# Weight block sums by adding transfers, four plain pairs first, and token operands in portions

## Chip, cores and metric

One core of a Trainium2 chip runs the whole program. The metric is the device time in microseconds (us), as the median of several executions. TensorE (PE in the profile) multiplies matrices, VectorE (DVE) and ScalarE (ACT) work element by element, GpSimd (POOL) too, and SyncE (SP) issues transfers between DRAM and the on-chip memory.

## What is computed

A two-layer bidirectional encoder trunk on 512 + 256 tokens with a model width of 1024. Each layer has a mixer (layer 0: HGRN2 and dilated window attention; layer 1: gated linear attention), then a gated convolutional feed-forward network (FFN), then a per-layer embedding added through a sigmoid gate. The change lies in the FFN alone, which runs once per layer:

```python
def _conv_ffn(x, w_up, conv_w, conv_b, w_down):   # x: RMS-normed, 1024 wide; w_up: 1024 x 5632
    u = x @ w_up
    up = jnp.pad(u, ((0, 0), (1, 1), (0, 0)))
    u = up[:, :-2] * conv_w[0] + up[:, 1:-1] * conv_w[1] + up[:, 2:] * conv_w[2] + conv_b
    a, gate = jnp.split(u, 2, axis=-1)
    return (a * jax.nn.gelu(gate, approximate=False)) @ w_down
```

## The kernel before

Activations lie transposed: 128 features on the partitions, the 768 tokens along a row. Every fp32 matrix product is made of three products of rounded parts: a value v is split into hi = round(v), made by ACT, and lo = v - hi, made by DVE, and TensorE adds w_hi x_hi, w_hi x_lo and w_lo x_hi.

Weights come in slabs of 128 x 1024 floats (512 KB) in a fixed list (`slabs`, built by `tail` at L1119 for the FFN). `prep` (L55) loads the next slab with SP (L72), makes hi on ACT (L73) and lo on DVE (L74). `slab` (L163) hands out a prepared slab and prepares one ahead. The tiles `raw`, `whi` and `wlo` have two buffers each, so hi and lo of a slab can be written when the products of the slab before the last are done. `proj` (L179) multiplies one slab with all tokens: 8 blocks x 3 parts x (512 + 256 columns), 48 matmuls in `gemm` (L177).

The up projection of the FFN needs 22 pairs of feature tiles, a linear one and a gate. The first NSTD = 2 pairs are plain: two slabs each, by `proj`, with evacuation into u on DVE (L965), times the norm factor R, which arrives late, after the first slab. The other 20 pairs use a Strassen-Winograd form of the 2 x 2 block product (two feature tiles, two halves of the 1024 inputs, two halves of the tokens) with seven products in place of eight: `seven` (L111), 7 x 12 = 84 matmuls of 386 columns each (L119), into three PSUM banks x, y, z. It needs

- sums of weight blocks: `prep_pair` (L78) loads two slabs (L81, L83), makes S1 and S3 on POOL (L97, L98), S2 and S4 on DVE (L99, L100), then splits the seven blocks in four operations on ACT and four on DVE (L90, L91);
- sums of token blocks: `operands(p)` (L933) scales two tiles of h by gain and R on DVE (L938) and calls `seven_operands` (L146): differences t1, t2 on DVE (L150, L152), t3, t4 on POOL (L151, L153), then four splits on ACT and DVE (L156, L157). It is called whole after each of the four plain projections, and a product of `seven` needs all four sets.

In `seven`, ACT copies the first and third product out (p1 L127, p5 L133), POOL adds them (L134), DVE makes u2 (L130), and four additions write u (L975, L978), after which POOL clears the gap columns between the two token groups (L977). `activate` (L953) follows whole: per half one ACT operation and two DVE taps (L947 to L950), Gelu on ACT, a product on DVE (L959). The down projection comes next: it splits each of the 22 results (`split`, L226, L227) and multiplies them in two passes of 11 slabs.

A scheduler makes each engine's instruction order at compile time, mainly by the order in the program among what it holds to be ready; an engine then runs its list strictly in that order. `bg` holds background generators; `tick`, called after each block or product, runs them on.

Of the kernel before, what the change touches and what calls it, by code (L numbers as in the profile page):

```python
# [13 lines left out]
ALU = mybir.AluOpType  # L14
# [21 lines left out]
HC = AC // 2  # L36
NSTD = 2
# [8 lines left out]
class Net:  # L46
# [8 lines left out]
    def prep(self, cut=1024, ahead=None):  # L55
        if self.sp >= len(self.slabs):
            return
        src = self.slabs[self.sp]
        self.sp += 1
        n = src.shape[-1]  # L60
        nc = self.nc
        if n == 2048:
            self.ready.append(self.prep_pair(src))
            return
# [12 lines left out]

    def prep_pair(self, src):  # L78
        nc = self.nc
        ra = self.wp.tile([128, 1024], F32, tag="raw", name="ra")  # L80
        nc.sync.dma_start(out=ra, in_=src[:, 0:1024])  # L81
        rb = self.wp.tile([128, 1024], F32, tag="raw", name="rb")
        nc.sync.dma_start(out=rb, in_=src[:, 1024:2048])  # L83
        a11, a12, a22, a21 = ra[:, 0:512], ra[:, 512:1024], rb[:, 0:512], rb[:, 512:1024]

        def parts(hpool, htag, lpool, ltag, r):
            n = r.shape[-1]
            hi = hpool.tile([128, 1024], F32R, tag=htag, bufs=2, name=htag)[:, :n]
            lo = lpool.tile([128, 1024], F32R, tag=ltag, bufs=2, name=ltag)[:, :n]
            nc.scalar.activation(hi, r, AF.Copy)  # L90
            nc.vector.tensor_tensor(out=lo, in0=r, in1=hi.bitcast(F32), op=ALU.subtract)  # L91
            return [[(hi[:, c:c + 128], lo[:, c:c + 128]) for c in range(c0, c0 + 512, 128)]
                    for c0 in range(0, n, 512)]
        sa = self.fp.tile([128, 1024], F32, tag="S", bufs=2, name="sa")
        sb = self.fp.tile([128, 1024], F32, tag="S", bufs=2, name="sb")
        s2, s1, s3, s4 = sa[:, 0:512], sa[:, 512:1024], sb[:, 0:512], sb[:, 512:1024]
# [4 lines left out]
        w = {}  # L101
        w["A11"], w["A12"] = parts(self.wp, "whi", self.wp, "wlo", ra)
        w["S2"], w["S1"] = parts(self.fp, "hs", self.fp, "ls", sa)
        w["S3"], w["S4"] = parts(self.fp, "hs", self.fp, "ls", sb)
        w["A22"], = parts(self.wp, "whi", self.wp, "wlo", rb[:, 0:512])
        return w
# [4 lines left out]
    def seven(self, X, c11, add):  # L111
        nc = self.nc
        W = self.slab()
        x, y, z = None, None, None
# [7 lines left out]
        pt = self.rp.tile([128, AC], F32, tag="Rt", name="p15")  # L122
        ug = self.rp.tile([128, AC], F32, tag="sq", name="ug")
        p1, p5, u2, g = pt[:, 0:HC], pt[:, HC:AC], ug[:, 0:HC], ug[:, HC:AC]
        x = self.mm()[:, 0:HC]
        prod(x, "A11", "B11", True)
        nc.scalar.copy(p1, x)  # L127
        y = self.mm()[:, 0:HC]
        prod(y, "S2", "T2", True)
        nc.vector.tensor_tensor(out=u2, in0=y, in1=p1, op=ALU.add)  # L130
        z = self.mm()[:, 0:HC]
        prod(z, "S1", "T1", True)
        nc.scalar.copy(p5, z)  # L133
        nc.gpsimd.tensor_tensor(out=g, in0=p1, in1=p5, op=ALU.add)  # L134
        prod(x, "A12", "B21", False)
        c11(x)
        prod(y, "S3", "T3", False)
        add(1, 1, y, g)
        prod(z, "S4", "B22", False)
        add(0, 1, z, u2)  # L140
        prod(y, "A22", "T4", False)
        add(1, 0, y, p1)
# [3 lines left out]
    def seven_operands(self, x1, x2, ta, tb, slots):  # L146
        nc = self.nc
        b11, b12, b21, b22 = x1[:, 0:HC], x1[:, HC:AC], x2[:, 0:HC], x2[:, HC:AC]
        t1, t2, t3, t4 = ta[:, 0:HC], ta[:, HC:AC], tb[:, 0:HC], tb[:, HC:AC]
        nc.vector.tensor_tensor(out=t1, in0=b12, in1=b11, op=ALU.subtract)  # L150
        nc.gpsimd.tensor_tensor(out=t3, in0=b22, in1=b12, op=ALU.subtract)  # L151
        nc.vector.tensor_tensor(out=t2, in0=b22, in1=t1, op=ALU.subtract)  # L152
        nc.gpsimd.tensor_tensor(out=t4, in0=b21, in1=t2, op=ALU.subtract)  # L153
        s11, h2, l2, ha, la, hb, lb = slots
        for hi, lo, v in ((s11[:, 0:HC], s11[:, HC:AC], b11), (ha, la, ta), (h2, l2, x2), (hb, lb, tb)):
            nc.scalar.activation(hi, v, AF.Copy)  # L156
            nc.vector.tensor_tensor(out=lo, in0=v, in1=hi.bitcast(F32), op=ALU.subtract)  # L157
        self.X["B11"].append((s11[:, 0:HC], s11[:, HC:AC]))
        for names, h, lo in ((("B21", "B22"), h2, l2), (("T1", "T2"), ha, la), (("T3", "T4"), hb, lb)):
            self.X[names[0]].append((h[:, 0:HC], lo[:, 0:HC]))  # L160
            self.X[names[1]].append((h[:, HC:AC], lo[:, HC:AC]))
# [748 lines left out]
    def ffn(self, l):  # L910
        nc, tc, a = self.nc, self.tc, self.a
        with tc.tile_pool(name=f"f{l}", bufs=1) as fp, \
# [10 lines left out]
            for k in range(KT):  # L923
                nc.sync.dma_start(out=hd[k], in_=self.h[k])
            for u in us:
# [4 lines left out]
            self.X = {n: [] for n in ("B11", "B21", "B22", "T1", "T2", "T3", "T4")}  # L930


            def operands(p):  # L933
                x1, x2 = aslot(2, f"xn{2 * p}", F32), aslot(3, f"xn{2 * p + 1}", F32)
                for k, x in ((2 * p, x1), (2 * p + 1, x2)):
                    nc.gpsimd.memset(x[:, TP:TP + GAP], 0.0)
                    for (c0, w), (uc, _) in zip(CH, ACOL):
                        nc.vector.scalar_tensor_tensor(out=x[:, uc:uc + w], in0=self.h[k][:, c0:c0 + w],  # L938
                                                       scalar=self.cols[:, C_FFN + 8 * l + k:C_FFN + 8 * l + k + 1],
                                                       in1=self.R[:, c0:c0 + w], op0=ALU.mult, op1=ALU.mult)  # L940
                tags = [(self.xp, f"x{p}"), (fp, f"xb{p}")] + [(self.xp, f"x{4 + 3 * p + i}") for i in range(3)] \
                    + [(self.hp, f"h{2 * p + i}") for i in range(2)]
                self.seven_operands(x1, x2, aslot(4, "ta", F32), aslot(5, "tb", F32),
                                    [pool.tile([128, AC], F32R, tag=t, name=t) for pool, t in tags])

            def conv_taps(c, u, f):
                nc.scalar.activation(c, u[:, 1:1 + AC], AF.Identity, scale=conv[:, f, 1:2], bias=conv[:, f, 3:4])  # L947
                nc.vector.scalar_tensor_tensor(out=c, in0=u[:, 0:AC], scalar=conv[:, f, 0:1], in1=c, op0=ALU.mult,
                                               op1=ALU.add)
                nc.vector.scalar_tensor_tensor(out=c, in0=u[:, 2:2 + AC], scalar=conv[:, f, 2:3], in1=c,  # L950
                                               op0=ALU.mult, op1=ALU.add)

            def activate(j, u):  # L953
                act[j] = aslot(j, f"act{j}", F32)
                c = fp.tile([128, AC], F32, tag="c", name="cg")
                conv_taps(act[j], u[0], j)
                conv_taps(c, u[1], NF + j)
                self.other(c, c, AF.Gelu)
                nc.vector.tensor_tensor(out=act[j], in0=act[j], in1=c, op=ALU.mult)  # L959
            for j in range(NSTD):  # L960
                for part in range(2):
                    n = 2 * j + part
                    pj = self.proj0(split=True) if n == 0 else self.proj()
# [3 lines left out]
                    if part == 1:  # L967
                        activate(j, us)
                    operands(n)
            for j in range(NSTD, NF):  # L970
                u = us

                def add(m, half, bank, other):
                    o = u[m][:, 1 + half * HC:1 + (half + 1) * HC]
                    nc.vector.tensor_tensor(out=o, in0=bank, in1=other, op=ALU.add)  # L975
                    if half:
# [286 lines left out]
```

## Time and profile before

| | us |
|---|---|
| median of 3 runs | 2387.71 |
| lowest and highest | 2387.23, 2389.49 |
| the profiled execution | 2386.55 |
| its span (first to last instruction) | 2384.8 |
| TensorE busy in it | 2291.9 |
| mean granted TensorE clock in it | 0.985 of full |

In the rows, an engine's busy time is the time in which it runs anything; "idle before" is the wait just ahead of an instruction, with the instruction that ended it. A name such as L99 is a line of the kernel. A granted clock of 1.00 is 2.4 GHz and of 0.50 is 1.2 GHz.

### The profile page before, as it was taken

Reading aid. Unit: us, or ns where it says so; the run is one execution under the profiler, and the core shown is the slowest. Engines: PE = TensorE matmul, PEld = TensorE weight load, DVE = VectorE, ACT = ScalarE, POOL = GpSimd, SP = SyncE. Lnnn points to the kernel's source line nnn. Section 1 sums busy time; section 2 is a strip of 40 time slices with the busy share of each in tenths; the row PEclk is TensorE's granted clock in tenths of the full one; section 3 lists DMA queues with packets and bytes.
Section 4 is the critical chain, followed back from the end, with each engine's and each line's share of the span. In section 5 each row is a group of like instructions: output and inputs, shape, how many; then the busy total and the mean of one; then the engine's idle time right before and its main releaser. Section 6 shows DMA issues by size and latency. Waiting matters only on the chain. (4 is left out here: it accounts for less than half of the span.)

```text
span 2384.8 us, 32943 instructions
## 1 busy us (share of the span) xinstructions
PE 2291.9 (96%) x13524; PEld 2083.2 (87%) x13524; DVE 1571.4 (66%) x2054; ACT 1052.1 (44%) x1422; POOL 247.6 (10%) x308
## 2 busy tenths in 40 slices
PE   8999999999995999999999999999968999999997
PEld 6989889898884999998888899998858999988887
DVE  7546355364548888895445687876478898864366
ACT  5333243332434454454334565655344555543353
POOL 1010010100103222220000000000032222200000
PEclk9999999999998999999999999999989999999999
DMA  4111111112230121223122311113311221231221
GB/s 160 54 54 36 54 45 45 54 45 73 93 107 31 63 69 64 71 71 115 62 76 76 106 54 36 36 36 113 111 44 54 71 71 64 70 115 65 75 87 53
DMA packets 50231, 165.70 MB, mean 69 GB/s; under 512 B 5696, under 2 KB 7744, under 8 KB 50080
## 3 DMA queue, kind: packets, MB, share of 16 engines
q1 hardware_dynamic: 48928, 162.02, 20.3%
q8 instruction: 106, 1.74, 0.3%
q10 hardware_dynamic: 1152, 1.57, 0.2%
q14 instruction: 45, 0.37, 0.1%
HBM read 150.99 MB, written 12.58 MB: 69 GB/s over the span
## 5 line engine op out<-in xcount | busy, mean ns | idle before, releaser
L177 PE MATMUL pj<-xh,whi 128*128 128x512 f32 (+1 forms) x2160 | 576.8, 348 | 9.2 <-ACT whi L73 6.1
L177 PE MATMUL pj<-xh,wlo 128*128 128x512 f32 (+1 forms) x2160 | 555.8, 339 | 22.0 <-DVE wlo L74 22.0
L177 PE MATMUL pj<-xl,whi 128*128 128x512 f32 (+1 forms) x2160 | 556.1, 338 | 2.7 <-DVE xl L233 2.7
L177 PEld LDWEIGHTS pj<-xh,wlo 128*128 128x128 f32 (+1 forms) x2160 | 331.6, 189 | 70.7 <-DVE wlo L74 22.7
L177 PEld LDWEIGHTS pj<-xl,whi 128*128 128x128 f32 (+1 forms) x2160 | 333.3, 189 | 52.6 <-DVE xl L233 4.5
L177 PEld LDWEIGHTS pj<-xh,whi 128*128 128x128 f32 (+1 forms) x2160 | 333.5, 190 | 50.7 <-ACT whi L73 6.1
L73 ACT ACTIVATE whi<-raw 128x1024 fp32r<-128x1024 f32 (+1 forms) x164 | 170.7, 1041 | 405.5 <-PE pj L177 387.6
L74 DVE TENSOR_TENSOR wlo<-raw,whi 128x1024 fp32r<-128x1024 f32 (+1 forms) x164 | 199.7, 1218 | 148.4 <-ACT whi L73 148.3
L119 PE MATMUL mm<-x,hs 128*128 128x386 f32 x800 | 221.7, 342 | 4.5 <-ACT hs L90 3.7
L119 PE MATMUL mm<-x,whi 128*128 128x386 f32 x480 | 139.8, 345 | 20.2 <-DVE x L157 15.8
L119 PEld LDWEIGHTS mm<-x,hs 128*128 128x128 f32 x800 | 147.9, 190 | 6.1 <-ACT hs L90 4.4
L227 DVE TENSOR_TENSOR xl<-act,xh 128x772 fp32r<-128x772 f32 x88 | 84.6, 968 | 69.3 <-ACT xh L226 69.3
L226 ACT ACTIVATE xh<-act 128x772 fp32r<-128x772 f32 x88 | 73.8, 843 | 95.4 <-PE pj L177 90.9
L119 PE MATMUL mm<-x,ls 128*128 128x386 f32 x320 | 109.5, 342 | 0.0
L119 PEld LDWEIGHTS mm<-x,whi 128*128 128x128 f32 x480 | 89.9, 191 | 21.9 <-DVE x L157 16.3
L357 ACT COPY kc<-X 128x768 f32<-128x768 f32 x56 | 50.5, 901 | 124.6 <-PE mm L344 68.2
L119 PE MATMUL mm<-h,whi 128*128 128x386 f32 x320 | 86.4, 351 | 17.4 <-DVE u L975 17.3
L99 DVE TENSOR_TENSOR sa<-sa,ra 128x512 f32<-128x512 f32 x40 | 69.7, 1743 | 44.2 <-POOL sa L97 44.2
L177 PE MATMUL mm<-xl,whi 128*128 128x512 f32 x352 | 90.6, 337 | 0.0
L177 PE MATMUL mm<-xh,whi 128*128 128x512 f32 x352 | 90.6, 337 | 0.0
L177 PE MATMUL mm<-xh,wlo 128*128 128x512 f32 x352 | 90.4, 338 | 0.0
L372 DVE COPY_PREDICATED A<-masks,mm 128x512 f32<-128x512 uint8 x112 | 60.8, 591 | 37.0 <-PE mm L344 36.9
(279 smaller groups left out, 4185.5 us busy)
## 6 DMA issues: line engine op xcount, KB each, us to landing
raw<-w_ev SPq DMA_DIRECT2D x55, 512.0 KB, 3.5
raw<-w_dn SPq DMA_DIRECT2D x44, 512.0 KB, 3.5
ra<-w_up SPq DMA_DIRECT2D x40, 512.0 KB, 3.7
rb<-w_up SPq DMA_DIRECT2D x40, 512.0 KB, 3.7
raw<-w_od SPq DMA_DIRECT2D x24, 512.0 KB, 3.4
hd<-h SPq DMA_DIRECT2D x24, 384.0 KB, 2.3
h<-hd SPq DMA_DIRECT2D x24, 384.0 KB, 5.3
raw<-w_pg SPq DMA_DIRECT2D x16, 512.0 KB, 3.5
```

The source lines that it names most:

```text
L73: nc.scalar.activation(hi[:, s], raw[:, s], AF.Copy)
L74: nc.vector.tensor_tensor(out=lo[:, s], in0=raw[:, s], in1=hi[:, s].bitcast(F32), op=ALU.subtract)
L99: nc.vector.tensor_tensor(out=s2, in0=s1, in1=a11, op=ALU.subtract)
L119: nc.tensor.matmul(bank, w, v, start=start and n == 0 and i == 0, stop=n == 3 and i == 2, skip_group_check=True)
L177: nc.tensor.matmul(o, w, x[:, c0:c0 + n], start=first and si == 0, stop=last and si == 2)
L226: nc.scalar.activation(xh[:, :n], src, AF.Copy)
L227: nc.vector.tensor_tensor(out=xl[:, :n], in0=src, in1=xh[:, :n].bitcast(F32), op=ALU.subtract)
L357: nc.scalar.copy(dst.rearrange("p (n c j) -> p n c j", c=2, j=h), src)
L372: nc.vector.copy_predicated(A[:, tl[0]:tl[0] + n, :], self.masks[:, li, :].unsqueeze(1).to_broadcast([128, n, 128]), p.rearrange("p (i t) ...
```

## The change

NSTD becomes 4 and HC, the half of the tokens, 384 instead of 386: the halves are now taken without the gap, and the second half is written into u in two pieces (128 and 256 columns).

Plain slabs of the up projection (tuples in the list): ACT makes hi and also -hi into lo, and a GpSimd transfer adds the slab from DRAM to lo.

Pairs: the weights are stored as four blocks of 128 x 512 (256 KB). `load_pair` loads two of them, and GpSimd transfers with `accum_op=ALU.add` form S1, S2, S3 and S4 in place, one after another in the same two buffers, each after the split of what lay there. The signs change so that sums suffice (N1, N2, N4 for T1, T2, T4); the gate half then comes out negated, which `nconv`, a negated copy of its taps, undoes. `split_pair` is a generator that splits one block per step; `split_step` takes a step after each product, so that blocks of the next pair are made during the products of this one. The order of products is now A11, S1, S2, A12, S3, S4, A22, and g is made on DVE straight from PSUM.

Token operands: `operands` scales h in place, in whole rows, makes all four differences on DVE, and yields between portions; `chain` runs it in the background, one portion for every two ticks from the second plain projection on. `activate` is a generator too, which runs during the next pair's products. The GpSimd descriptor memory goes from 1024 to 4096 bytes.

```diff
@@ prep
+        added = type(src) is tuple
...
             nc.sync.dma_start(out=raw[:, s], in_=src[:, s])
             nc.scalar.activation(hi[:, s], raw[:, s], AF.Copy)
-            nc.vector.tensor_tensor(out=lo[:, s], in0=raw[:, s], in1=hi[:, s].bitcast(F32), op=ALU.subtract)
+            if added:
+                nc.scalar.activation(lo[:, s], raw[:, s], AF.Copy, scale=-1.0)
+                nc.gpsimd.dma_start(out=lo[:, s], in_=src[:, s], accum_op=ALU.add)
+            else:
+                nc.vector.tensor_tensor(out=lo[:, s], in0=raw[:, s], in1=hi[:, s].bitcast(F32), op=ALU.subtract)
...
-        nc.gpsimd.tensor_tensor(out=s1, in0=a21, in1=a22, op=ALU.add)
-        nc.gpsimd.tensor_tensor(out=s3, in0=a11, in1=a21, op=ALU.subtract)
-        nc.vector.tensor_tensor(out=s2, in0=s1, in1=a11, op=ALU.subtract)
-        nc.vector.tensor_tensor(out=s4, in0=a12, in1=s2, op=ALU.subtract)
...
+    def load_pair(self, src):
+        r = self.wp.tile([128, 1024], F32, tag="raw", name="ra")
+        a, s = r[:, 0:512], r[:, 512:1024]
+        nc.sync.dma_start(out=s, in_=src[2])
+        nc.sync.dma_start(out=a, in_=src[0])
+        nc.gpsimd.dma_start(out=s, in_=src[3], accum_op=ALU.add)
+        return src, a, s
...
+    def split_pair(self, load, w):
+        src, a, s = load
+        a12 = self.load_block(src[1])
...
+            nc.scalar.activation(hi, r, AF.Copy)
             nc.vector.tensor_tensor(out=lo, in0=r, in1=hi.bitcast(F32), op=ALU.subtract)
...
+        parts("S1", s, 0, 0)
+        nc.gpsimd.dma_start(out=s, in_=src[0], accum_op=ALU.add)
+        yield
+        parts("A11", a, 0, 1)
+        nc.gpsimd.dma_start(out=a, in_=src[2], accum_op=ALU.add)
+        yield
+        parts("A12", a12, None, 0)
+        a22 = self.load_block(src[3])
+        yield
+        parts("S2", s, None, 0)
+        nc.gpsimd.dma_start(out=s, in_=src[1], accum_op=ALU.add)
+        yield
+        parts("S3", a, 1, 0)
+        yield
+        parts("S4", s, 1, 1)
+        yield
+        parts("A22", a22, None, 0)
+        yield
...
+    def next_pair(self):
+        self.psplit = None
+        if self.ploads:
+            w = {}
+            self.pw.append(w)
+            self.psplit = self.split_pair(self.ploads.pop(0), w)
+            if self.psrc:
+                self.ploads.append(self.load_pair(self.psrc.pop(0)))
...
+    def seven(self, c11, add):
+        def after():
             self.tick()
+            self.split_step()
...
             for j in range(NSTD):
                 for part in range(2):
                     n = 2 * j + part
+                    if n == 1:
+                        self.spawn(chain())
+                    if n == 2 * NSTD - 1:
+                        self.pairs([a["w_up2"][l, i] for i in range(NSTD, NF)])
                     pj = self.proj0(split=True) if n == 0 else self.proj()
...
                     if part == 1:
-                        activate(j, us)
-                    operands(n)
+                        run(activate(j, us, False))
+            self.drain()
+            for _ in range(5):
+                self.split_step()
             for j in range(NSTD, NF):
...
+                self.seven(lambda bank: nc.scalar.copy(us[0][:, 1:1 + HC], bank), add)
+                self.spawn(activate(j, us, True))
+            self.drain()
```

## Rows read from the trace of the kernel before

**Rows 1.** The page: busy time (share) by engine, TensorE's busy tenths in 40 slices.

```profile
PE 2291.9 (96%) x13524; PEld 2083.2 (87%) x13524; DVE 1571.4 (66%) x2054; ACT 1052.1 (44%) x1422; POOL 247.6 (10%) x308
...
PE   8999999999995999999999999999968999999997
```

**Rows 2.** Windows of both up projections: length, busy us (instructions) by engine, clock, DMA.

```profile
core 0: us, PE busy (x) PEld busy (x) DVE busy (x) ACT busy (x) POOL busy (x), PEclk, DMA share, GB/s
702.60:784.00 81.40, 55.56 (x276) 48.01 (x276) 63.79 (x82) 34.92 (x43) 25.18 (x21) 0.83 0.13 43
784.00:1081.40 297.40, 287.67 (x1604) 281.92 (x1603) 266.05 (x289) 152.83 (x198) 73.89 (x94) 1.00 0.21 68
1725.20:1800.00 74.80, 49.72 (x244) 42.37 (x243) 60.77 (x79) 32.65 (x40) 23.66 (x19) 0.82 0.12 41
1800.00:2101.20 301.20, 293.56 (x1637) 287.80 (x1636) 269.41 (x293) 155.47 (x200) 75.38 (x96) 1.00 0.21 69
```

**Rows 3.** Windows without a TensorE wait: one in the pairs, one in plain slabs.

```profile
1835.80:1850.40 14.60, 14.60 (x83) 14.60 (x84) 12.56 (x14) 7.31 (x10) 3.92 (x4) 1.00 0.23 72
1100.00:1260.00 160.00, 160.00 (x917) 139.73 (x916) 65.89 (x70) 54.04 (x62) 0.00 (x0) 1.00 0.20 68
```

**Rows 4.** TensorE's waits from 640 to 1300 us: us in total, times, longest.

```profile
PE pj L177 <- DVE wlo L74: 11.0, 1, 11.0
PE mm L119 <- DVE u L975: 9.7, 18, 1.7
PE mm L119 <- DVE x L157: 7.9, 1, 7.9
```

**Rows 5.** DVE's timeline at layer 0's head: start, us, operation [idle before <- releaser].

```profile
702.96 0.95 DVE L476 TENSOR_TENSOR h<-h,pj 128x768 f32<-128x768 f32 x1 [4.47 <-PE pj L177]
...
717.60 1.02 DVE L965 TENSOR_TENSOR u<-pj,R 128x512 f32<-128x512 f32 x2
...
740.30 0.96 DVE L157 TENSOR_TENSOR h<-tb,h 128x772 fp32r<-128x772 f32 x1 [2.75 <-ACT h L156]
741.18 1.22 DVE L74 TENSOR_TENSOR wlo<-raw,whi 128x1024 fp32r<-128x1024 f32 x1
```

**Rows 6.** POOL's timeline there: the subtraction ahead of that wait.

```profile
733.69 4.72 POOL L151 TENSOR_TENSOR tb<-xn,xn 128x386 f32<-128x386 f32 x1 [8.07 <-DVE xn L938]
```

**Rows 7.** DVE's groups from 800 to 1060 us: busy us, mean ns | idle before.

```profile
L99 DVE TENSOR_TENSOR sa<-sa,ra 128x512 f32<-128x512 f32 x17 | 29.9, 1762 | 19.8 <-POOL sa L97 19.8
L959 DVE TENSOR_TENSOR act<-act,cg 128x772 f32<-128x772 f32 x17 | 27.6, 1626 | 0.0
...
L948 DVE SCALAR_TENSOR_TENSOR act<-u,conv,act 128x772 f32<-128x772 f32 x17 | 17.3, 1020 | 0.8 <-ACT act L947 0.6
...
L975 DVE TENSOR_TENSOR u<-mm,ug 128x386 f32<-128x386 f32 x32 | 16.3, 548 | 0.0
L91 DVE TENSOR_TENSOR wlo<-rb,whi 128x512 fp32r<-128x512 f32 x17 | 11.8, 692 | 2.0 <-ACT whi L90 1.1
```

**Rows 8.** DVE's groups from 717 to 769 us, the head of layer 0.

```profile
L157 DVE TENSOR_TENSOR x<-xn,xb 128x772 fp32r<-128x772 f32 x3 | 2.9, 956 | 0.0
L965 DVE TENSOR_TENSOR u<-pj,R 128x512 f32<-128x512 f32 x4 | 2.7, 687 | 0.0
...
L959 DVE TENSOR_TENSOR act<-act,cg 128x772 f32<-128x772 f32 x2 | 1.9, 954 | 0.0
...
L965 DVE TENSOR_TENSOR u<-pj,R 128x256 f32<-128x256 f32 x4 | 1.7, 417 | 0.0
```

**Rows 9.** ACT's groups of splits over the span, by shape.

```profile
L73 ACT ACTIVATE whi<-raw 128x1024 fp32r<-128x1024 f32 x159 | 168.2, 1058 | 402.4 <-PE pj L177 384.4 <-issue 16.7 <-PE mm L177 1.0
...
L90 ACT ACTIVATE whi<-rb 128x512 fp32r<-128x512 f32 x40 | 25.3, 633 | 19.8 <-PE mm L119 19.6
```

**Rows 10.** DMA issues: count, KB each, median us from issue to landing.

```profile
ra<-w_up SPq DMA_DIRECT2D x40, 512.0 KB, 3.7
...
h<-hd SPq DMA_DIRECT2D x24, 384.0 KB, 5.3
...
yT<-y SPq DMA_DIRECT2D x4, 256.0 KB, 2.2
```

More of the change, by code (lines that the diff above doesn't have):

```diff
@@ L105, in prep_pair @@
-        w["A22"], = parts(self.wp, "whi", self.wp, "wlo", rb[:, 0:512])
-        return w
-    def seven(self, X, c11, add):
+            w[name] = [(hi[:, c:c + 128], lo[:, c:c + 128]) for c in range(0, 512, 128)]
+        parts("S1", s, 0, 0)
[6 more added lines that the diff above has]
+        a22 = self.load_block(src[3])
@@ L112, in seven, with split_step @@
+    def split_step(self):
+        if self.psplit is not None and next(self.psplit, 0) == 0:
+            self.next_pair()
+            if self.psplit is not None:
+                next(self.psplit)
+            elif self.slabs[self.sp] is None:
+                self.sp += 1
+                self.prep()
+    def seven(self, c11, add):
         nc = self.nc
-        W = self.slab()
-        x, y, z = None, None, None
+        X, W = self.X, self.pw.pop(0)
         def prod(bank, a, b, start):
@@ L125, in seven @@
         x = self.mm()[:, 0:HC]
         prod(x, "A11", "B11", True)
-        nc.scalar.copy(p1, x)
-        y = self.mm()[:, 0:HC]
[L129 to L134, printed above, removed]
+        nc.scalar.copy(q1, x)
+        after()
+        z = self.mm()[:, 0:HC]
+        prod(z, "S1", "N1", True)
@@ L135, in seven @@
+        nc.vector.tensor_tensor(out=g, in0=z, in1=q1, op=ALU.add)
+        after()
+        y = self.mm()[:, 0:HC]
+        prod(y, "S2", "N2", True)
+        nc.vector.tensor_tensor(out=u2, in0=y, in1=q1, op=ALU.add)
+        after()
         prod(x, "A12", "B21", False)
         c11(x)
+        after()
         prod(y, "S3", "T3", False)
         add(1, 1, y, g)
+        after()
         prod(z, "S4", "B22", False)
         add(0, 1, z, u2)
-        prod(y, "A22", "T4", False)
-        add(1, 0, y, p1)
+        after()
@@ L146, in seven_operands @@
+        prod(y, "A22", "N4", False)
+        add(1, 0, y, q1)
+        after()
     def seven_operands(self, x1, x2, ta, tb, slots):
         nc = self.nc
[L148 to L152, printed above, removed]
@@ new lines, in seven_operands @@
+        yield
+        nc.vector.tensor_tensor(out=t3, in0=b22, in1=b12, op=ALU.subtract)
+        nc.vector.scalar_tensor_tensor(out=n4, in0=n2, scalar=-1.0, in1=b21, op0=ALU.mult, op1=ALU.subtract)
+        high(hb, tb)
+        yield
+        low(s11[:, 0:HC], s11[:, HC:T], b11)
+        low(h2, l2, x2)
+        yield
+        low(ha, la, ta)
+        low(hb, lb, tb)
+        yield
+        self.X["B11"].append((s11[:, 0:HC], s11[:, HC:T]))
+        for names, h, lo in ((("B21", "B22"), h2, l2), (("N1", "N2"), ha, la), (("T3", "N4"), hb, lb)):
@@ new lines, in operands, with conv_taps @@
+                tags = [(self.xp, f"x{4 * p + i}") for i in range(4)]
+                tags += [(self.hp, f"h{2 * p - 2 + i}") if p else (fp, f"xb{4 + i}") for i in range(2)]
+                tags.append((fp, f"xb{p}"))
+                yield from self.seven_operands(
+                    hs[0], hs[1], aslot(4, "ta", F32)[:, :T], aslot(5, "tb", F32)[:, :T],
+                    [lambda pool=pool, t=t: pool.tile([128, T], F32R, tag=t, name=t) for pool, t in tags])
+            def conv_taps(c, u, w, f, bias):
+                nc.scalar.activation(c, u[:, 1:1 + AC], AF.Identity, scale=w[:, f, 1:2], bias=bias)
+                yield
+                for o, i in ((0, 0), (2, 2)):
+                    nc.vector.scalar_tensor_tensor(out=c, in0=u[:, o:o + AC], scalar=w[:, f, i:i + 1], in1=c,
+                                                   op0=ALU.mult, op1=ALU.add)
+                    yield
@@ new lines, in activate @@
+            def activate(j, u, negated):
+                act[j] = aslot(j, f"act{j}", F32)
+                if negated:
+                    c = self.hp.tile([128, AC], F32, tag="h6", name="cg")
+                else:
+                    c = self.rp.tile([128, AC], F32, tag="sq", name="cg")
+                gbias = conv[:, NF + j, 3:4]
+                gate = conv_taps(c, u[1], *((nconv, j, gbias) if negated else (conv, NF + j, gbias)))
+                lin = conv_taps(act[j], u[0], conv, j, conv[:, j, 3:4])
+                next(gate), next(lin)
+                for g in (lin, gate):
+                    for _ in g:
+                        yield 1
@@ L958, in activate, with run, chain @@
                 self.other(c, c, AF.Gelu)
+                yield 1
                 nc.vector.tensor_tensor(out=act[j], in0=act[j], in1=c, op=ALU.mult)
+            def run(gen):
+                for _ in gen:
+                    pass
+            def chain():
+                for p in range(KT // 2):
+                    for _ in operands(p):
+                        yield 2
             for j in range(NSTD):
```

123 lines of the change are left out of this document (54 added, 69 removed).

## Prediction

> **What bounds the kernel now.** Read the page's shares first: TensorE is busy nearly all the time and the other engines are not, so a saving elsewhere counts only where TensorE waits or runs at half clock. The slices show two such places besides the ends: the 13th slice, and the 30th and 31st [rows 1]. Then windows over each layer's up projection, cut from where the last output projection leaves TensorE to the first down matmul: the hole is at the head, with a granted clock of 0.83 and 0.82, and behind it comes a long stretch at full clock in which DVE is busy 266 of 297 us and ACT only 153 [rows 2].
>
> TensorE's price of work comes from stretches without a hole: 160 us hold 917 matmuls of alternately 512 and 256 columns, so 0.1745 us each and 48 x 0.1745 = 8.37 us per plain slab; 14.6 us hold 83 of 386 columns, so 0.176 us each and 84 x 0.176 = 14.8 us per pair of slabs in the seven-product form [rows 3]. The losses of the four windows of rows 2 follow. Layer 0's head has 276 matmuls, 192 of the four plain slabs and 84 of pairs: 33.5 + 14.8 = 48.3 us of work in 81.4 us, lost 33.1. Layer 1's head: 244, so 33.5 + 52 x 0.176 = 42.7 in 74.8, lost 32.1. The rest: 1604 x 0.176 = 282.3 in 297.4, lost 15.1; 1637 x 0.176 = 288.1 in 301.2, lost 13.1. In all 93.4 us: 65.2 in the heads (waiting, and running slowly after waiting), 28.2 in the steady stretches.
>
> Who causes them? In layer 0 TensorE waits 11.0 us for one weight remainder (wlo, L74), 7.9 us for the last token operand (L157), and 18 times about half a microsecond for an addition into u (L975) [rows 4]; layer 1 has the same three. The late wlo had its input long before, but stands on DVE behind a whole call of operands(), which waits for ACT, which waits for a POOL subtraction of 4.72 us [rows 5, 6]. In the steady stretch DVE is held by the same engine: L99 takes 1.76 us where a 512-column operation of its kind takes 0.69, L959 1.63 where it takes 0.95 without POOL beside it [rows 7, 8].
>
> **The change, part by part.** Arithmetic on TensorE: four plain slabs more and two pairs fewer per layer, and 384 columns for 386 (between the two prices of rows 3, whose pair of 512 and 256 averages 384 too: 0.1752). Needed before 4 x 8.37 + 20 x 14.78 = 329.2; after 8 x 8.37 + 18 x 84 x 0.1752 = 67.0 + 264.9 = 331.9. This costs 2.7 us per layer, 5.4 in all, and is on the path. With every wait gone the gain is 93.4 - 5.4 = 88.0 us, and the time 2387.7 - 88.0 = 2299.7. (Profiled execution: 2386.55, of which 2384.8 is span; 1.2 below the median of three, so differences are simply taken from the median.)
>
> Plain slabs. The DVE subtraction (1.22 us, rows 5) goes; ACT makes a negated copy (1.06 us, rows 9), and a GpSimd transfer of 512 KB adds the weights to it. For slab n+1 this starts when slab n starts, since the two hi and lo buffers come free then: two ACT operations 2.1 us, then the transfer, and 8.37 us until TensorE wants it. So it is hidden up to X of about 6.0 us from issue to landing. No accumulating transfer and none issued by GpSimd is in the trace. Bounds: 3.7 us, a plain load of that size, and twice that, 7.4, since its target is read as well; I take 5.3, the row of a slow load in company [rows 10]. One ACT operation ahead in the queue (about 1 us) then makes it 0.3 late, 2 us per layer for seven slabs; at 7.4 it is 2.4 late, 17 us per layer. What the removal costs if this cover fails is just that. Behind a waiting GpSimd queue stand only later accumulations, as its subtractions and memsets are gone.
>
> Heads. DVE's work there, by row durations [rows 7, 8, 5]: eight evacuations of 0.69 + 0.42, 8.8 us; four activations of 4 x 1.02 + 0.95, 20.1; four operand sets, each two scalings, four 384-column differences at 0.55 and remainders of 0.55 + 3 x 0.96 (about 7.6), 30.6. Sum 59.5, startable at 717.6, when R is there [rows 5]; without the last activation and evacuation, 53.4, so done by about 771.0. The eight plain slabs last until 702.6 + 67.0 = 769.6. The operands are cut into portions in the order of the projections, so an evacuation stands behind at most four portions, and no POOL result is waited for any more. So the 11.0 and 7.9 us go, and with them the low clock. What is late next: the first pair's blocks, behind DVE's last work of the stage: 0 to 6 us, I take 3.
>
> Steady stretch. DVE per pair: before 1.76 + 0.69 + three remainders of 1.22 and one of 0.69 + four additions of 0.55 + taps 4.08 + 1.63 = 14.7 of a 15.6 us period (14.8 of work and 15.1 lost over 19 pairs). After: seven remainders of 0.69, four PSUM additions of which two are cut into 128 and 256 columns (together 2 x 0.55 + 0.55 + 2 x 0.70), taps 4.08, product 0.95: 12.9 of 14.7 us. ACT gets shorter, more operations, at 0.63 [rows 9], and is half idle. The new thing is a chain through one buffer: load S1's block, add, split S1, add, split S2, add, split S4. The step of S2 comes three products (6.3 us) after that of S1, S4's two products (4.2 us) after S2's. A split takes 0.63 + 0.69 = 1.3 us; let a 256 KB accumulation take L from readiness to landing, with GpSimd's issue in it. Bounds: 2.2, a one-way transfer of that size, and 7.4 [rows 10] (GpSimd's price for issuing is not shown, which is why the upper end stays). I take twice 2.2, 4.4. Then S4's split waits 1.3 + 4.4 - 4.2 = 1.5 us at the head of ACT's queue, DVE's remainder behind it, and then q1, u2 and the additions that free PSUM. TensorE wants S4 only at product six, 10 us later, and an addition has one product, 2.1 us, of slack; DVE has 14.7 - 12.9 = 1.8 us to catch up. So it is covered, barely: 0 to the present 0.7 us per pair, I take 0.15, 2.7 us per layer.
>
> The rule of the Trainium skill for this price (DMA: Bandwidth & Descriptors, Anatomy of one DMA) is a fixed 2.0 us plus bytes over 436 GB/s for a GpSimd-issued transfer, that is 2.6 us for 256 KB and 3.2 for 512 KB as estimates by that page. By it neither chain waits, the residue falls to the first-pair delay and the tail, and the sum would be 2308; no run so far shows such a transfer.
>
> Small edits: the gap memsets leave POOL, which nobody misses. Scaling h in place waits for its store to DRAM, issued with the last output projection, 14 us ahead of R [rows 5]. The activations spread over the next pair's products give u back after four of seven ticks; u is written again from product four on. The down projection's first operand slots now come free at the last pair's product six instead of one: one product hides about 2 us of ACT and DVE, I take 1 us per layer (0 to 3).
>
> Sum per layer: 2 + 3 + 2.7 + 1 = 8.7, for two 17.4. **Forecast 2299.7 + 17.4 = 2317 us.** With all upper ends, 2 x (17 + 6 + 13 + 3) = 78 us: 2378.
>
> **The rivals.** (1) Nothing waits: 2296 to 2305. For it: every step has slack on paper, and 2.2 is a shown time. Against: four places with under 2 us to spare. (2) The accumulations land late but not very (X and L near 7): 7.4 costs 34 us in the plain slabs and perhaps 20 in pairs: 2335 to 2383. For it: GpSimd needs 4.72 us for one 386-column subtraction in rows 6, and its queue issues all of these in order. (3) Slower: the chain becomes the period. There are two raw buffers, so one load (3.7), three splits (3.9) and three accumulations must fit in two pairs: 7.6 + 3L = 2P. It bounds TensorE from L = 7.3 us on; the gain is used up where 67 + 6 + 18P equals the present 377 (mean of 378.8 and 376.0), P = 16.9, so from L = 8.7 us. At 10 us P is 18.8 and the time 2388 + 36 x 1.9 = 2456. Against it: 8.7 is more than twice the time of a 512 KB load. The same page's rule to move 1 MiB or more per DMA (Rules for kernel authors) also speaks against cutting two 512 KB loads into eight transfers: its fixed 2.0 us eight times is 16 us per pair if none overlaps, an estimate near this rival; the DMA share of 0.21 in rows 2 says that the engines themselves have room. (4) It doesn't do what it says: the order on DVE and ACT still puts a block behind long waits, so a head keeps half its loss. That is again 2335 to 2365 and is counted in (2).
>
> **How the numbers follow.** Forecast case, 2305 to 2335: 0.56. Rival 1: 0.12. Rivals 2 and 4: 0.15. Within 0.2% of 2387.7 (plus or minus 4.8 us, about what can be told from no change): 0.03. Rival 3: 0.14. Faster is 0.56 + 0.12 + 0.15 = 0.83. The range 2296 to 2365 holds the first two and two thirds of the third, 0.78.
>
> **What would show it.** Right: heads without a TensorE wait over 3 us, granted clock 1.0 in them, no DVE row of 1.7 us, a period per pair near 14.9 us, and up projections near 341 us (before 378.8 and 376.0). Wrong: TensorE waiting for a transfer into wlo in each plain slab (X); ACT waiting for a transfer at S4 or S2 for more than 4 us and a period above 15.6 (L); or the first pair waiting over 6 us for DVE (order).

## The result, and the profile after

The changed kernel takes 2418.03 us, the median of four runs (2413.81 to 2424.18), beside 2387.52 of the kernel before on the same chip: a ratio of 1.0128, with a 95% interval of 1.0105 to 1.0151. It is slower, by 1.3%. The profiled run, the longest of the four, took 2424.18 us, of which 2422.4 are span.

The page of the kernel after, as in [rows 1] (busy time, share and instructions by engine; TensorE's busy tenths in 40 slices), with the GpSimd queue's packets, MB and share of the 16 DMA engines, and two groups of DMA issues with the median us from issue to landing:

```profile
PE 2309.7 (95%) x13572; PEld 2083.5 (86%) x13572; DVE 1455.3 (60%) x2166; ACT 1042.1 (43%) x1492; POOL 188.9 (8%) x236
...
PE   8999999999999888889999999999998888899997
...
q0 software_dynamic: 23040, 46.15, 12.1%
...
ra<-w_up POOLq DMA_DIRECT2D x144, 256.0 KB, 4.3
...
wlo<-w_up POOLq DMA_DIRECT2D x16, 512.0 KB, 7.6
```

The 5 and the 6 of [rows 1] are gone. In their place TensorE runs at 8 tenths all through the pairs. The work that was to be taken off DVE is off it (1455.3 us of busy time for 1571.4 before), and the kernel is longer all the same.

Windows over layer 0's up projection, with the columns of [rows 2]: the eight plain slabs, the 18 pairs, and a stretch inside the pairs.

```profile
703.30:777.70 74.40, 70.83 (x390) 60.61 (x389) 57.49 (x81) 41.95 (x51) 9.48 (x11) 0.98 0.55 122
777.70:1096.90 319.20, 280.77 (x1514) 268.70 (x1513) 212.25 (x343) 139.94 (x222) 59.29 (x68) 0.98 0.57 118
850.00:1060.00 210.00, 182.84 (x981) 174.42 (x980) 139.62 (x225) 89.29 (x143) 41.58 (x48) 0.98 0.59 119
```

The head came out nearly as forecast: the clock stays at 0.98 where it was 0.83, and the eight slabs take 74.4 us for 67.0 of work. The pairs did not: 319.2 us for the 264.9 of the prediction's arithmetic. In the trace one pair follows another every 17.75 us (ACT's copy of product one starts at 853.62 and, eight pairs on, at 995.59), where it was 15.6; over both layers, without the first period of each, the mean is 17.9. Layer 1's pairs take 321.2 us (1817.8 to 2139.0). So the pairs lose 54 to 56 us per layer, spread over all of them.

Waits of TensorE and of ACT over the span (what waited, on what: us in total, times, longest):

```profile
PE mm L167 <- DVE ug L186: 58.1, 34, 1.9
PE mm L167 <- DVE u L1072: 17.2, 24, 2.7
PE pj L249 <- DMA wlo<-w_up: 9.2, 8, 2.7
PE mm L167 <- DVE ug L182: 2.8, 2, 1.6
...
ACT whi L112 <- DMA ra<-w_up: 145.8, 64, 3.5
ACT hs L112 <- DMA ra<-w_up: 130.6, 36, 5.6
```

TensorE waits in 34 of the 36 pairs for u2 (L186), a small addition on DVE, and never for a weight block of a pair. But ACT stands 276.4 us for adding transfers, 7.7 us per pair. How a wait of ACT for a weight block becomes a wait of TensorE for u2 is seen in the timelines of one period (start, us, operation [idle before <- releaser]). ACT first; the first line and the last are the split of S4 in two pairs, `hs<-ra` is that of S2, `x2` those of S1 and A11:

```profile
902.85 0.63 ACT L112 ACTIVATE whi<-ra 128x512 fp32r<-128x512 f32 x1 [3.22 <-DMA ra<-w_up]
...
906.91 0.46 ACT L178 COPY q<-mm 128x384 f32<-128x384 f32 x1
907.27 1.15 ACT L112 ACTIVATE whi<-ra 128x512 fp32r<-128x512 f32 x2
...
914.56 0.63 ACT L112 ACTIVATE hs<-ra 128x512 fp32r<-128x512 f32 x1 [3.33 <-DMA ra<-w_up]
917.78 0.63 ACT L112 ACTIVATE whi<-ra 128x512 fp32r<-128x512 f32 x1 [2.59 <-DMA ra<-w_up]
920.29 0.63 ACT L112 ACTIVATE whi<-ra 128x512 fp32r<-128x512 f32 x1 [1.88 <-DMA ra<-w_up]
```

DVE in the same period:

```profile
903.52 0.69 DVE L113 TENSOR_TENSOR wlo<-ra,whi 128x512 fp32r<-128x512 f32 x1 [3.16 <-ACT whi L112]
904.44 1.02 DVE L1024 SCALAR_TENSOR_TENSOR act<-u,conv,act 128x772 f32<-128x772 f32 x1 [0.23 <-ACT act L1021]
905.38 0.55 DVE L1072 TENSOR_TENSOR u<-mm,q 128x384 f32<-128x384 f32 x1
905.85 1.02 DVE L1024 SCALAR_TENSOR_TENSOR act<-u,conv,act 128x772 f32<-128x772 f32 x1
906.78 0.69 DVE L113 TENSOR_TENSOR ls<-rb,hs 128x512 fp32r<-128x512 f32 x1
907.38 2.08 DVE L1024 SCALAR_TENSOR_TENSOR cg<-u,nconv,cg 128x772 f32<-128x772 f32 x2
909.37 0.55 DVE L182 TENSOR_TENSOR ug<-mm,q 128x384 f32<-128x384 f32 x1
909.84 1.28 DVE L113 TENSOR_TENSOR wlo<-ra,whi 128x512 fp32r<-128x512 f32 x2
911.04 0.55 DVE L186 TENSOR_TENSOR ug<-mm,q 128x384 f32<-128x384 f32 x1
...
915.22 0.69 DVE L113 TENSOR_TENSOR ls<-ra,hs 128x512 fp32r<-128x512 f32 x1 [2.16 <-PE mm L167]
```

And POOL, which issues the adding transfers for S2 (L116), S3 (L119) and S4 (L125):

```profile
910.82 0.86 POOL L116 DMA_DIRECT2D ra<-w_up  x1 [2.59 <-DVE wlo L113]
911.42 1.15 POOL L119 DMA_DIRECT2D ra<-w_up  x1
916.21 0.86 POOL L125 DMA_DIRECT2D ra<-w_up  x1 [3.64 <-DVE ls L113]
```

Read across: at 902.85 the sum S4 has landed and ACT splits it. DVE subtracts its remainder, and then works off what stands behind that in its list: two taps with the addition into u between them, A22's remainder, two gate taps, g. Only then comes the remainder of the next pair's S1, done at 910.5. POOL may now add S2's block into that buffer; it lands for ACT at 914.56, 4.0 us later. S2's remainder is done at 915.91, POOL issues S4's addition, and that lands at 920.29, 4.4 us later. There stands the next S4, 17.44 us after the first. It is a closed loop: nothing in it waits for TensorE, and TensorE can't run faster than it. (The matmul that the view names as releaser of S2's remainder, at 915.22, is not one: ACT's split of S2 ends at 915.19, and in 33 other waits of this kind the view names that split.) u2 and g are merely the results in DVE's list that come late behind it.

Less the two landings, 4.03 and 4.38 us, this period holds 9.03 us of work. In each of the 32 periods that follow the first of a layer the trace has 9.02 or 9.03 us of it, while the landings vary (means 4.35 and 4.55). After its wait for u2 TensorE ran partly at the lower clock in the period shown (0.57 granted from 912 to 915), and that period is still one of the shortest.

### The profile page after: what moved, and what is told of

The parts are those of the page before. It is cut to its first block, busy times and chain, and to the rows that moved or that the text cites. A ratio compares the mean times of both kernels' runs of the same rounds, so it can differ in the third digit from the quotient of the medians.

```text
span 2422.4 us, 33496 instructions
## 1 busy us (share of the span) xinstructions
PE 2309.7 (95%) x13572; PEld 2083.5 (86%) x13572; DVE 1455.3 (60%) x2166; ACT 1042.1 (43%) x1492; POOL 188.9 (8%) x236
## 3 DMA queue, kind: packets, MB, share of 16 engines
q0 software_dynamic: 23040, 46.15, 12.1%
## 4 chain that ended last, share of the span: by engine, by line
PE 65%; DMA 16%; issue 11%; DVE 5%; ACT 2%; POOL 1%; POOLq 0%; SPq 0%; DVEq 0%; ACTq 0%
PE pj L249 43%; DMA ra<-w_up 14%; PE mm L249 11%; PE mm L416 4%; PE mm L498 2%; DMA wlo<-w_up 1%; DVE wlo L113 1%; PE mm L859 1%; DVE ls L113 1%; POOL ra L90 1%; PE mm L167 1%; PE mm L466 1%; ACT hs L112 1%; ACT whi L112 1%; DVE act L1024 1%
## 5 line engine op out<-in xcount | busy, mean ns | idle before, releaser
L249 PE MATMUL pj<-xh,whi 128*128 128x512 f32 x2288 | 610.1, 348 | 9.1 <-ACT whi L73 6.0
L249 PE MATMUL pj<-xh,wlo 128*128 128x512 f32 x2288 | 588.7, 339 | 9.2 <-DMA wlo<-w_up 9.2
L249 PE MATMUL pj<-xl,whi 128*128 128x512 f32 x2288 | 589.7, 339 | 2.5 <-DVE xl L305 2.4
L249 PEld LDWEIGHTS pj<-xh,wlo 128*128 128x128 f32 x2288 | 351.2, 189 | 62.5 <-DMA wlo<-w_up 11.7
L249 PEld LDWEIGHTS pj<-xl,whi 128*128 128x128 f32 x2288 | 353.6, 189 | 55.6 <-DVE xl L305 4.6
L249 PEld LDWEIGHTS pj<-xh,whi 128*128 128x128 f32 x2288 | 353.1, 190 | 53.2 <-ACT whi L73 6.0
L78 DVE TENSOR_TENSOR wlo<-raw,whi 128x1024 fp32r<-128x1024 f32 (+2 forms) x156 | 190.1, 1218 | 137.2 <-ACT whi L73 137.2
L167 PE MATMUL mm<-x,whi 128*128 128x384 f32 x720 | 200.4, 344 | 2.8 <-DVE ug L182 2.8
L167 PE MATMUL mm<-x,wlo 128*128 128x384 f32 x432 | 146.8, 340 | 0.0
L167 PE MATMUL mm<-x,hs 128*128 128x384 f32 x432 | 123.9, 341 | 1.0 <-ACT q L178 0.7
```

What stands on the lines that cost most here:

```text
L249: nc.tensor.matmul(o, w, x[:, c0:c0 + n], start=first and si == 0, stop=last and si == 2)
```

## The experiments

Two theories went into the first runs. The loop: the period is two landings (S2's and S4's) plus the fixed work between them, and the transfers for S1 and S3 are not on it. The rate: the adding transfers are too many for their queue, and each of the four costs about its quarter. Differences are taken from the 2418.0 us after and the 2387.5 before. The windows shown below are all of 850 to 1060 us, where the kernel after has 981 matmuls in 210 us; a pair has 84, so 210 x 84 over the count is the period, 18.0 us for that kernel. A time without an interval is one execution; the four of the kernel after lie 10 us apart, so a few us between two such times say nothing.

**All four sums left out** (no_sums). The four GpSimd transfers of each pair are removed, and nothing else:

```diff
-        nc.gpsimd.dma_start(out=s, in_=src[3], accum_op=ALU.add)
...
-        nc.gpsimd.dma_start(out=s, in_=src[0], accum_op=ALU.add)
...
-        nc.gpsimd.dma_start(out=a, in_=src[2], accum_op=ALU.add)
...
-        nc.gpsimd.dma_start(out=s, in_=src[1], accum_op=ALU.add)
```

> The four adding transfers of every pair are left out, so S1 to S4 hold single blocks; all else stays, the plain slabs' adding transfers too. Both theories expect the pairs to run freely: loop theory (two adding transfers stand in series once per pair in ACT's and DVE's order lists) and rate theory (GpSimd's queue or the 16 DMA engines can't carry the added transfers in one pair's time) give a period of 15.0 to 15.3 us in place of 17.75, and 2418 - 36 x 2.6 = 2324 us (2315 to 2335). If it stays above 2370, neither holds and the order of products and evacuations is at fault.

It took 2307.49 us, and the window reads

```profile
850.00:1060.00 210.00, 210.00 (x1201) 207.47 (x1200) 167.69 (x262) 111.56 (x168) 0.00 (x0) 1.00 0.26 81
```

TensorE never stops in this window: a period of 14.7 us, and a time 8 us below the expected range. Without the sums the changed kernel takes 80 us less than the kernel before; the sums as transfers cost 110.5.

**S4's sum alone left out** (no_s4_sum), then **S3's alone** (no_s3_sum): the line with `src[1]`, or that with `src[2]` into `a`, is removed.

> Only the third adding transfer into the buffer of S1 (the one that makes S4 from S2) is left out of every pair, 1 of 4. Loop theory: the loop loses one landing and its wait, about 4.1 us of 17.75, so the period falls to what else bounds, 15.0 to 15.5, and the time to about 2418 - 36 x 2.4 = 2332 us (2320 to 2345). Rate theory: a quarter of the added transfers goes, so about a quarter of the 2.9 us that a pair lost: 2418 - 36 x 0.7 = 2392 us (2380 to 2405).

> Only the adding transfer that makes S3 (into the other buffer) is left out of every pair, again 1 of 4, the same bytes as in no_s4_sum. It is in nobody's series. Loop theory: period 17.75 less at most 0.3 us for GpSimd's issue, 2407 to 2420 us. Rate theory: as no_s4_sum, 2392 us (2380 to 2405).

They took 2337.39 and 2415.96 us. The windows, S4's first:

```profile
850.00:1060.00 210.00, 206.42 (x1165) 202.44 (x1164) 163.44 (x263) 109.38 (x167) 32.01 (x37) 1.00 0.55 125
```

```profile
850.00:1060.00 210.00, 183.13 (x985) 175.15 (x983) 138.90 (x227) 89.77 (x144) 30.62 (x36) 0.98 0.49 104
```

Both kernels issue 108 adding transfers in place of 144. One is 81 us faster, the other 2, which is within the spread. The rate theory falls; which transfer it is decides.

Without S4's sum the period by the count is 15.1 us and not yet 14.7. There ACT waits for S3's transfer, and S4's split stands right behind S3's. In 30 of 34 periods it is 8.8 us from S3's split round to the next A11's remainder, behind which that transfer is issued, and the way on to S3's next split, 6.3 us on average, is the rest. So a second loop, through S3's transfer, stands just above TensorE's own time.

**The same transfers, without the adding** (plain_transfers): `accum_op` is dropped from the four (one is shown), so they are as many, as large and in the same order.

```diff
-        nc.gpsimd.dma_start(out=s, in_=src[0], accum_op=ALU.add)
+        nc.gpsimd.dma_start(out=s, in_=src[0])
```

> The changed kernel with its four transfers per pair as plain ones of the same size from the same queue: a block replaces what it should be added to, so the sums are left out of the computation; the order, the waits and the engines' work are unchanged. It measures what the adding itself costs. The loop through the lists passes two landings per pair (3.74 and 4.08 us from the issue to the split). If most of that is the addition, a plain transfer takes about the 2.9 us of the plain loads beside it, the period falls by 2 x 1.0 us and the time to about 2418 - 36 x 2.0 = 2346. If the landing is the issue and the way, not the addition, it is within 15 us of 2418.

It took 2335.07 us. Their issues, and ACT's timeline, S4, S2 and S4 again:

```profile
ra<-w_up POOLq DMA_DIRECT2D x144, 256.0 KB, 3.0
```

```profile
900.68 0.63 ACT L112 ACTIVATE whi<-ra 128x512 fp32r<-128x512 f32 x1 [1.82 <-DMA ra<-w_up]
...
911.37 0.63 ACT L112 ACTIVATE hs<-ra 128x512 fp32r<-128x512 f32 x1 [1.78 <-DMA ra<-w_up]
...
915.79 0.63 ACT L112 ACTIVATE whi<-ra 128x512 fp32r<-128x512 f32 x1 [1.34 <-DMA ra<-w_up]
```

This period is 15.11 us. The remainder of S1 ends at 908.36 and that of S2 at 912.73, so the two landings are 3.01 and 3.06 us: 6.07 of 15.11, which leaves 9.04 of work. In the kernel after they are 4.03 and 4.38: 8.41 of 17.44, which leaves 9.03. The same holds over the whole trace: in each of the 32 later periods of this kernel too the work is 9.02 or 9.03 us, and the mean period of 15.6 us is that plus landings of 3.18 and 3.36. So over both kernels the period is 9.03 us plus two landings, measured, and by these means an adding transfer of 256 KB is 1.2 us longer on the way than a plain one.

**S2's and S4's sums by DVE** (dve_s2_s4): the two transfers on the loop become additions of 512 columns in place, the two off the loop stay.

```diff
-        nc.gpsimd.dma_start(out=s, in_=src[0], accum_op=ALU.add)
...
+        nc.vector.tensor_tensor(out=s, in0=s, in1=a, op=ALU.add)
         nc.gpsimd.dma_start(out=a, in_=src[2], accum_op=ALU.add)
...
-        nc.gpsimd.dma_start(out=s, in_=src[1], accum_op=ALU.add)
...
+        nc.vector.tensor_tensor(out=s, in0=s, in1=a12, op=ALU.add)
         parts("S4", s, 1, 1)
```

> The changed kernel, with the sums of S2 and S4 made by DVE in place (two additions of 0.69 us per pair) and only S1's and S3's by adding transfers, which are off the series. Loop theory: no landing is left in ACT's and DVE's series, DVE has 12.9 + 1.4 = 14.3 of 14.7 us by mean durations, so a period of 14.8 to 15.3 and 2307.5 (no_sums) + 36 x 0.3 = 2318 us (2308 to 2335), under both kernels. If DVE's load is what binds as in the kernel before, the period is 15.5 and the time 2337.

It took 2313.93 us, 0.9697 of the time before (0.968 to 0.9713): faster than both kernels.

```profile
850.00:1060.00 210.00, 210.00 (x1200) 207.91 (x1200) 183.15 (x289) 112.30 (x170) 19.88 (x23) 1.00 0.46 112
```

DVE is busier than in the kernel after (183 us for 140, in more pairs) and TensorE never waits in this window. The time is 6 us above that without any sum, and 104 us below that with S2's and S4's sums as transfers.

**S4's sum alone by DVE** (dve_s4).

> As the changed kernel, but S4's sum alone is made by DVE in place, S2's stays an adding transfer. Loop theory: one landing stays in the series, so it is no_s4_sum (2337) plus 0.69 us of DVE per pair that its wait mostly covers: 2335 to 2355. It must lie above dve_s2_s4 if the landing counts more than an addition on DVE, below it if DVE's load does.

2329.88 us, 5 below the expected range, and above dve_s2_s4, as it must be if the landing counts more than an addition on DVE. The window has 1165 matmuls, as in the run without that sum: with one landing and one addition of 0.69 us the loop is 9.03 + 4.03 + 0.69 = 13.8 us, below TensorE's 14.7. It still waits 12.5 us, in 17 pieces, for additions into u; whether the second loop, through S3's transfer, is behind these too was not separated.

**The loop's order moved** (s4_behind_q1, s4_last): S4's split on ACT is held back until the copy q1 is issued; or the steps of S4 and A22 are exchanged.

```diff
+        with self.tc.issue_after(self.q1i.ins):
+            parts("S4", s, 1, 1)
-        parts("S4", s, 1, 1)
```

> The changed kernel with one edge of order and no other work: ACT's split of S4 may stand in its list only behind the copy of the first product (q1) of the same pair. All four adding transfers stay. Loop theory with the order as its part: q1 and the taps no longer wait for S4's landing but run during it, so some 3 us of the 6.3 us of DVE work between S4 and the next S1 leave the loop: period 15.0 to 16.2, 2418 - 36 x 2.2 = 2340 us (2325 to 2365). If the landings alone make the loop, whatever stands between them, the time stays within 10 us of 2418.

> The changed kernel with two steps of the series exchanged: A22 is split before S4, so that S4's landing has a product more. Loop theory: about 1 us (A22's split) moves from between S4 and the next S1 into S4's wait, period 16.7, 2418 - 36 x 1.0 = 2382 us (2370 to 2400). If steps in program order set the spacing, S4 gains a whole product, 2.1 us: 2343 us (2335 to 2360). If the compiled order ignores the exchange, 2418.

The exchange changed nothing: 2423.05 us, and in the compiled order of ACT S4's split stood where it had stood. Holding S4 back gave 2388.08 us, 30 less, which lies between what the theories expected. ACT's timeline there, S2, S3, then S4 with S1 and A11 of the next pair:

```profile
908.47 0.63 ACT L112 ACTIVATE hs<-ra 128x512 fp32r<-128x512 f32 x1 [2.64 <-DMA ra<-w_up]
...
913.41 0.64 ACT L112 ACTIVATE whi<-ra 128x512 fp32r<-128x512 f32 x1 [3.94 <-DMA ra<-w_up]
...
917.82 1.68 ACT L112 ACTIVATE whi<-ra 128x512 fp32r<-128x512 f32 x3
```

S4's split no longer waits, since its transfer has the time until q1. But S3's now waits longest. The period shown is 16.6 us, that by the window's 1035 matmuls 17.0, and it is the second loop, through A11's remainder, S3's transfer and the splits of S3 and S4: in 28 of 34 periods all of it but the way from A11's remainder to S3's split is 9.21 or 9.22 us. S3's transfer was issued at 906.6, so ACT stood for it until almost 7 us after its issue, with another adding transfer issued half a microsecond ahead of it. Such company goes with its lateness: from issue to landing S3's transfer takes 7.0 us here and 5.6 in the kernel after (medians), in both nearly always right behind another adding transfer, and 4.0 in dve_s2_s4, where as a rule none is issued just ahead of it. Its size is the same in all three.

**The plain half alone** (four_plain): the kernel before with four plain pairs (eight slabs), its four operand sets still whole behind the first four projections, and no adding transfer.

```diff
-NSTD = 2
+NSTD = 4
...
-                    operands(n)
+                    if n < KT // 2:
+                        operands(n)
```

> The kernel before with four plain pairs instead of two, and nothing else: the operand sets stand whole behind the first four plain projections, as before. TensorE gets 2.7 us more work per layer. If the heads' loss came from too little plain work beside the operand sets, half to two thirds of the 65 us goes: 2387.5 - 40 + 5 = 2352 us (2335 to 2370). If it came from the whole operand sets on DVE's list ahead of a slab's remainder, the 11 us waits stay and it is 2387.5 - 15 + 5 = 2377 us (2370 to 2395).

2368.27 us, 0.9925 of before (0.9909 to 0.9942): between the two values expected, and at the upper end of the first one's range. Two of its waits of TensorE:

```profile
PE pj L177 <- DVE wlo L74: 32.1, 4, 13.0
PE mm L119 <- DVE u L976: 15.0, 34, 0.7
```

The remainder of a plain slab still stands behind whole operand sets, for up to 13.0 us. So four plain pairs alone do not fill the head. With the new form of the operands they do (the head of dve_s2_s4_lo below); whether by its portions or by its four differences on DVE, where POOL made two, was not separated.

**The plain remainders back on DVE as well** (dve_s2_s4_lo): dve_s2_s4, with the subtraction in place of the negated copy and the 512 KB transfer.

```diff
-            if added:
+            if False:
```

> S2's and S4's sums by VectorE as in the run that was faster than both kernels (2313.9 us), and besides the low half of each plain slab is again VectorE's subtraction, without the negated copy and the 512 KB transfer. There TensorE waited 9.1 us, 10 times, for that transfer. If the transfer is the worse way, the waits go and the time is 2300 to 2310. If VectorE is the bound of the stage's head (59.5 us of work there by the prediction, and 8 x 1.22 = 9.8 us more for the subtractions, in 67 us of plain slabs), TensorE waits for VectorE instead, for a remainder or for the first pair: 2314 to 2340.

2308.85 us, 0.9675 of before (0.9658 to 0.9691): 5 us better again, and the fastest of those that compute the whole. Windows of its head and its pairs in layer 0, and TensorE's one kind of wait between 695 and 1100 us:

```profile
703.00:770.00 67.00, 67.00 (x386) 58.61 (x385) 60.95 (x84) 34.34 (x42) 1.89 (x2) 1.00 0.27 75
770.00:1040.60 270.60, 267.06 (x1514) 266.06 (x1513) 237.06 (x385) 142.54 (x223) 29.37 (x34) 0.99 0.47 107
```

```profile
PE mm L167 <- DVE wlo L113: 3.4, 2, 2.3
```

The eight slabs take 67.0 us to the tenth. DVE then is a little late with the first pair, whose stretch is 4.7 us longer than in dve_s2_s4 (270.6 for 265.9). So both expectations held in part: in layer 0 the transfer cost 7.7 us in the head (74.7 us for the eight slabs in dve_s2_s4), DVE's subtractions 4.7 behind it.

Not run: a third raw buffer, which would have tested the prediction's two-buffer rule by itself.

## Why the prediction was wrong

**What bounds the kernel before, and what its waits are worth.** Right. The floor, 2299.7 us, says what is left when no wait is. The fastest run's profiled execution, 2308.7, has one loss that its rows show, the 4.7 us at the first pair; twice that on the floor is 2309.1. One reading beside the sum is not borne out: both rows of L959 at 0.95 us [rows 8] ran beside a POOL subtraction (the first from 734.85 us, inside that of [rows 6]), so they do not show the operation "without POOL beside it". The sum does not need it: the product took 0.96 us in the kernel after, at 912.11. And the four additions from PSUM are five, as the sum itself counts them.

**TensorE's arithmetic.** Right: 67.0 us for eight plain slabs against a window of 67.00, and 264.9 for 18 pairs against 265.9 in dve_s2_s4.

**Heads.** Right in the kernel after: the first pair starts straight behind the last slab, and no wait there is over 3 us. The 0 to 6 us at the first pair, 3 taken, came only with the remainders on DVE, as 4.7.

**Plain slabs.** What waits was right, TensorE for the transfer into wlo, but both sizes were off: 7.6 us from issue to landing where 5.3 was taken, just over the upper bound of 7.4, and less lateness from it than the sum's rule gives. By that rule 7.6 us is 2.6 late for each of seven slabs, 18 us; the head lost 7.4 us of 74.4, where 2 were charged. The difference is 5 us per layer, 10 in all. The rule of the Trainium skill (DMA: Bandwidth & Descriptors, Anatomy of one DMA), 2.0 us plus the bytes at 436 GB/s, gives 3.2 us for 512 KB and 2.6 for 256, as estimates by that page. Here these transfers took 7.6 and 4.3, so by it the sum would have been further off; the plain 256 KB transfer of the same queue, at 3.0, is near to it. The same page's rule to move 1 MiB or more per transfer (Rules for kernel authors) spoke for rival 3, and the time went that way, but not for its reason: plain_transfers has all eight small transfers per pair and a mean period of 15.6, and what is slow is two that wait for each other.

**Price of a pair's transfer.** Right: 4.4 was taken, and 4.0 and 4.4 measured in the period shown, 4.35 and 4.55 on average. It stayed far under the 7.3 from which rival 3 was to bind.

**The pairs: here the prediction failed.** Two sentences did it. The first costed S4's wait as 1.5 us, from steps that lie three and two products apart, as though each block came round with TensorE. In the trace ACT stands at S2, S3 and S4 for 3.3, 2.6 and 1.9 us, since these splits stand in ACT's list in fixed order, with little between S3's and S4's, and what runs late in one pair is not given back: the next pair's S1 stands behind this pair's S4, on ACT and on DVE. The text named what is queued behind S4's split (q1, u2 and the additions) but not S1's remainder, which releases the next transfer and closes the loop. The second is the rule of rival 3, that with two raw buffers "one load (3.7), three splits (3.9) and three accumulations must fit in two pairs". It closed the loop through the buffers, and so gave the chain two periods. S1's split at 907.27 did not wait for a transfer: the buffers were in time. The loop through the lists is passed once in every pair, with two landings in it. So the sign that was to show it, ACT standing over 4 us at S4 or S2, did not come in the period shown, while the period passed 15.6.

The order of the lists is read here from the trace after; with it, the length of the loop comes out of the rows of before. On DVE from S4's remainder to S1's: three remainders of 0.69, four taps of 1.02, an addition and g at 0.55 [rows 7]; on ACT S4's split and S2's at 0.63 [rows 9], and S2's remainder. The sum is 2.07 + 4.08 + 1.10 + 1.26 + 0.69 = 9.2 us, and 9.03 was measured. With the prediction's own 4.4 per landing the period is 9.2 + 8.8 = 18.0, for 17.9 measured. By the prediction's own formula, 67 + 6 + 18P against 377, that is 397 us per layer and 2428 in all. Break-even at P = 16.9 lies at a landing of 3.9 us, not 8.7. So with the right loop the same prices would have given slower, and rival 3 would have been the forecast.

In numbers: the sum foresaw 340.6 us for layer 0's up projection, and it took 393.6. Of the 53.0 us, 2.4 are in the head (7.4 lost, 5 charged), and 50.6 in the pairs (319.2 against 264.9 + 2.7 + 1). Twice the 53.0, 106, is the distance from the forecast of 2317 to the profiled 2424 but for a microsecond. Of the 3 us per pair, TensorE's waits make 78.1 / 36 = 2.2; the rest is matmuls that run slower: 182.84 us for 981 in the window, 0.186 each, where dve_s2_s4 has 0.175. The granted clock, 0.98 for 1.00, would alone make it 0.179 (an estimate from that ratio); what makes the rest of that difference is open.

**What the range left out.** 2365 was too low by 53 us, as rival 3 was given 0.14 and a loss only past an L of 8.7.

## What to carry to other kernels

Before a cost is hidden "because its consumer comes later", write down each engine's list in order and follow every release through it until it comes back to its start: a chain of transfers that passes through in-order lists once per iteration sets the period when it is longer than the busiest engine's own work, however idle the engines on it are (here 9.03 us of work and two landings against TensorE's 14.7). That more buffers would not shorten it is argued from the lists, not shown. When one loop is cut, look for the next: here it ran through S3's transfer. Put an asynchronous step of several microseconds where it is passed once, off that loop (with S1's and S3's left as transfers TensorE never waited in the window shown), and give the steps on it to an engine that finishes in 0.7 us, even the busiest one beside TensorE. A saving of busy time on an engine is worth only the waits that its rows show ending on it.

## What the runs showed of the hardware

- An adding transfer that GpSimd issues took 4.3 us from issue to landing for 256 KB, and 7.6 for 512 KB, beside other traffic. The same 256 KB without the adding took 3.0, and SyncE's plain loads beside it 2.9 to 3.3.
- The adding showed elsewhere too: GpSimd's own issuing operation took 0.86 us, and 0.54 without it; the queue handled 23040 packets and held 12.1% of the DMA engines' time, and 13824 and 7.1% with plain transfers in the pairs, for the same 46.15 MB. Without the pairs' transfers it handled 2304 (no_sums), so each of the 144 makes 144 packets with the adding and 80 without.
- An adding transfer issued straight behind another landed later: in the period shown ACT saw S3's, issued at 911.42, 5.2 us after its issue operation ended, and those of S2 and S4 2.9 and 3.2 us after theirs. The medians from issue to landing are 5.6, 3.9 and 4.2 us, and S3's is 4.0 in dve_s2_s4, where S2's is not issued ahead of it. The plain ones take 3.0, 2.8 and 2.9 in the same places.
